# A decoder layer in split fp32: the high halves of 16 up-projection chunks come by a casting DMA of GpSimd's

## The chip, the cores and the metric

One core of a Trainium2 chip runs one launch of the kernel; the other cores are idle. The metric is the device time of one execution in microseconds (us), and for the kernel before it is the median of 2 runs. Profiles are of one execution each. Engines are named PE (TensorE, matmuls), ACT (ScalarE), DVE (VectorE), POOL (GpSimd) and SP (SyncE, which here only issues DMAs). PEld is TensorE's loading of its stationary operand.

## The reference, cut to what matters

One layer of a hybrid decoder over 256 tokens of width 1024, float32 in and out: a mixer of two branches (a chunkwise matrix memory and block attention), a layer norm, a gated feed-forward block, and a second layer norm. The change touches the feed-forward block:

```python
def conv_gated_mlp(x, w_up, conv_ffn, w_down):
    u = causal_dwconv(jnp.einsum("bsd,df->bsf", x, w_up), conv_ffn)
    g, up = jnp.split(u, 2, axis=-1)
    return jnp.einsum("bsf,fd->bsd", jax.nn.silu(g) * up, w_down)

# reference(), for its one layer
x = layer_norm(ALPHA * x + mix, ln1_g[l], ln1_b[l])
ffn = conv_gated_mlp(x, w_up[l], conv_ffn[l], w_down[l])
x = layer_norm(ALPHA * x + ffn, ln2_g[l], ln2_b[l])
```

`w_up` is 1024 x 5632 (gate and value, 2816 columns each), `w_down` 2816 x 1024, and the convolution is causal with three taps per channel.

## The kernel before, in words

**Split operands.** Matmuls run on float32r operands, a rounded form of float32. To keep float32 accuracy, each operand is cut in two: a high half, the value cast to float32r, and a low half, the value minus its high half. One product is three matmuls (`mm3`, L126: high x high L129, and the two mixed products L130 and L131). `split_into` (L91) makes the halves: ACT casts the high half (L93), DVE subtracts to get the low half (L94).

**Chunks.** All weights come from HBM as one stream of chunks of 128 partitions x 2048 float32 (1 MiB, 8 KB for each partition), in the order of `chunk_order` (L45). An "up" chunk holds 128 gate columns and 128 value columns of `w_up`; there are 22, up 0 to up 21. A "dn" chunk holds 256 rows of `w_down`; there are 11. From up 4 on they go in rounds: dn 0, up 4, up 5, dn 1, up 6, up 7, and so on to dn 7, up 18, up 19, and then up 20, up 21, dn 8, dn 9, dn 10. The first matmuls of dn d take the hidden chunks of up 2d and 2d + 1.

**Buffers.** `load` (L84) issues one chunk's DMA on SP's queue into a `raw` tile; there are three raw tiles, three `wh` tiles (high halves) and three `wl` tiles (low halves). `split_parts` (L100) takes a raw tile and a pair of `wh` and `wl`, cuts the 2048 columns into pieces (two of 1024 for most chunks), and returns one closure for each piece that calls `split_into`. A tile's next user waits until the last reader of the previous one is done: for `wh` and `wl` that is the matmuls of the chunk three before.

**The main loop** (in `run`) takes one chunk s per step. It emits the elementwise work of the step before and the split of chunk s + 2, then the load of chunk s + 5, then the matmuls of chunk s:

```python
self.elem_work(s, [] if late else self.split_parts(s + 2))
self.load(s + 5)
...
getattr(self, "step_" + kind)(s, i)
```

The order on each engine is the order of emission; every engine runs its own list and waits on semaphores. In a step after an up chunk the elementwise list is `[conv, None, None, gate]`, and the two pieces of the split take the places of the two `None`. `conv` is two ACT scalings (L1045) out of PSUM and four DVE multiply-adds (L1049). `gate` is a Silu on ACT (L1056), a product on DVE (L1057), and the split of the hidden chunk into `hh` (ACT) and `hl` (DVE). In a step after a dn chunk there is only the split.

**GpSimd** has few instructions here: two DMAs for the rows of the second layer norm (`load_ln_rows`, L843, emitted in the gate of up 5) and a power with one column in each layer norm (L949).

Of the kernel before, what the change touches and what calls it, by code (L numbers as in the profile page):

```python
# [10 lines left out]
F32 = mybir.dt.float32  # L11
F32R = mybir.dt.float32r
# [6 lines left out]
P = 128  # L19
# [13 lines left out]
WCOLS = KT * 264 + 64  # L33
# [27 lines left out]
def shift(kind, i):  # L61

    if kind in ("vm", "vb", "o"):
        return 48
    if kind in ("wa", "wb"):
        return 56
    if kind == "dn":

        return 40
    return 0 if kind == "wo" else 16  # L70


class Kernel:
# [10 lines left out]
    def load(self, s):  # L84
# [3 lines left out]
        self.nc.sync.dma_start(t, self.wst[s])  # L88
        self.raw[s] = t

    def split_into(self, wh, wl, raw):  # L91

        self.nc.scalar.copy(wh, raw)  # L93
        self.nc.vector.tensor_sub(wl, raw, wh.bitcast(F32))  # L94
# [5 lines left out]
    def split_parts(self, s):  # L100
        if s >= len(self.order) or s in self.w:
            return []
        raw = self.raw.pop(s)
        if s in self.extra:
            wh, wl = self.extra.pop(s)
            a = 8
        else:
            wh = self.stream.tile([P, WCOLS], F32R, tag="wh", name=f"wh{s}", bufs=3)
            wl = self.stream.tile([P, WCOLS], F32R, tag="wl", name=f"wl{s}", bufs=3)
            a = shift(*self.order[s])  # L110

        e, z, n, _ = odd(*self.order[s])
        wh, wl = (t[:, a - e:a + 2048 + z] for t in (wh, wl))
        edges = sorted({0, 256 if e else 0, 1024, 2048 - n, 2048})
        cuts = [(*(t[:, self.col(s, b):self.col(s, b) + d - b] for t in (wh, wl)), raw[:, b:d])
                for b, d in zip(edges, edges[1:])]
        self.w[s] = (wh, wl)
        return [lambda c=c: self.split_into(*c) for c in cuts]

    def col(self, s, c):  # L120
# [1027 lines left out]
def odd(kind, i):  # L1148

    if kind == "kb":  # L1150
        return 0, 8, 128, False
    if kind == "ga" and i < NG - 1:
        return 0, 8, 128, True
    if (kind, i) == ("up", 2):
        return 0, 8, 256, True
    if (kind, i) in (("vb", 3), ("up", 0), ("up", 1)):
        return 8, 0, 0, False
    return 0, 0, 0, False
# [78 lines left out]
```

## Time and profile before

| | |
|---|---|
| median of 2 runs | 486.95 us (486.84 to 487.06) |
| span of the profiled execution, first to last instruction | 484.5 us |
| granted TensorE clock, mean | 0.995 |
| busy: PE, PEld, DVE, ACT, POOL | 475.0, 459.4, 370.8, 288.1, 27.4 us |
| DMA moved | 94.29 MB, 195 GB/s over the span |

The profiled execution has a span only; its own time with what lies around the span isn't listed apart, and the median of the runs is 2.45 us above the span. A row of groups reads: line, engine, operation, output <- inputs, shapes, count | busy us, mean ns of one | idle time of the engine before them and what ended it. A row of the timeline gives start, length (us), engine, line, operation and count, and in brackets how long the engine stood idle before it and what released it. A row of DMA issues ends with the median us from issue to landing.

### The profile page before, as it was taken

How to read it: one execution, taken by the hardware profiler on the slowest of the kernel's cores; microseconds unless marked ns; L12 is line 12 of the kernel's file. 1: busy time of each engine (PE TensorE's matmuls, PEld its weight loads, DVE VectorE, ACT ScalarE, POOL GpSimd, SP SyncE). 2: the span in 40 equal slices, each digit the busy share in tenths (PEclk: the TensorE clock that was granted, in tenths of full speed). 3: DMA queues.
4: the chain of work that ended last, by engine and by line, in shares of the span. 5: the costliest groups of instructions: out<-in, count | busy, mean ns of one | idle time of the engine just before them, and what ended most of it. 6: DMA issues, size and time to landing. Idle time of an engine off the chain costs nothing.

```text
span 484.5 us, 9423 instructions
## 1 busy us (share of the span) xinstructions
PE 475.0 (98%) x3832; PEld 459.4 (95%) x3832; DVE 370.8 (77%) x681; ACT 288.1 (59%) x499; POOL 27.4 (6%) x43
## 2 busy tenths in 40 slices
PE   8999999999999999999999999999999999999993
PEld 6999999999999999999999999999999999999983
DVE  4877986897689668985677798878668666866877
ACT  5578876686667666866654623766456545654530
POOL 0501011001100110002000001000000000000000
PEclk9999999999999999999999999999999999999998
DMA  7986676375536562653954581827464545465202
GB/s 219 315 295 178 219 264 202 114 268 191 212 116 244 193 211 93 239 203 112 379 206 173 180 342 45 305 87 261 175 224 170 215 175 197 172 220 192 88 1 88
DMA packets 20918, 94.29 MB, mean 195 GB/s; under 512 B 4837, under 2 KB 7793, under 8 KB 11017
## 3 DMA queue, kind: packets, MB, share of 16 engines
q1 hardware_dynamic: 16714, 87.61, 50.9%
q0 software_dynamic: 4160, 6.07, 4.1%
q8 instruction: 30, 0.49, 0.4%
q14 instruction: 14, 0.11, 0.1%
HBM read 92.58 MB, written 2.64 MB: 197 GB/s over the span
## 4 chain that ended last, share of the span: by engine, by line
PE 97%; DMA 1%; DVE 1%; SPq 0%; issue 0%; ACT 0%; DVEq 0%
PE ps_up L131 8%; PE ps_up L129 8%; PE ps_up L130 8%; PE ffn L131 4%; PE ffn L130 4%; PE ffn L129 4%; PE ps_qm L129 2%; PE ps_vb L130 2%; PE ps_vb L131 2%; PE ps_vb L129 2%; PE ps_wb L131 2%; PE ps_ga L130 2%; PE mix L131 2%; PE ps_ga L131 2%; PE ps_kb L131 2%; PE ps_wa L131 2%
## 5 line engine op out<-in xcount | busy, mean ns | idle before, releaser
L94 DVE TENSOR_TENSOR wl<-raw,wh 128x1024 fp32r<-128x1024 f32 (+4 forms) x163 | 181.3, 1154 | 27.6 <-ACT wh L93 27.0
L93 ACT CAST wh<-raw 128x1024 fp32r<-128x1024 f32 (+4 forms) x163 | 153.1, 993 | 7.8 <-DMA raw<-in_wst_dram 4.6
L129 PE MATMUL ps_up<-x1h,wh 128*128 128x256 f32 x320 | 88.5, 277 | 0.0
L131 PE MATMUL ps_up<-x1h,wl 128*128 128x256 f32 x320 | 88.5, 277 | 0.0
L130 PE MATMUL ps_up<-x1l,wh 128*128 128x256 f32 x320 | 88.4, 276 | 0.0
L129 PEld LDWEIGHTS ps_up<-x1h,wh 128*128 128x128 f32 x320 | 60.2, 188 | 0.3
L130 PEld LDWEIGHTS ps_up<-x1l,wh 128*128 128x128 f32 x320 | 60.1, 188 | 0.4
L131 PEld LDWEIGHTS ps_up<-x1h,wl 128*128 128x128 f32 x320 | 60.1, 188 | 0.0
L1049 DVE SCALAR_TENSOR_TENSOR cu<-ps_up,vec,cu 128x255 f32<-128x255 f32 (+1 forms) x80 | 33.1, 476 | 23.5 <-ACT cu L1045 23.5
L131 PE MATMUL ffn<-wh,hl 128*128 128x512 f32 (+1 forms) x94 | 35.5, 378 | 0.0
L130 PE MATMUL ffn<-wl,hh 128*128 128x512 f32 (+1 forms) x94 | 35.5, 377 | 0.0
L129 PE MATMUL ffn<-wh,hh 128*128 128x512 f32 (+1 forms) x94 | 35.3, 375 | 0.0
L93 ACT CAST hh<-cu 128x256 fp32r<-128x256 f32 x22 | 8.9, 407 | 43.0 <-DVE cu L1057 43.0
L1045 ACT ACTIVATE cu<-ps_up,vec 128x256 f32<-128x256 f32 x40 | 16.7, 469 | 26.1 <-PE ps_up L131 26.1
L131 PEld LDWEIGHTS ffn<-wh,hl 128*128 128x128 f32 x94 | 17.7, 188 | 3.2
L130 PEld LDWEIGHTS ffn<-wl,hh 128*128 128x128 f32 x94 | 17.7, 188 | 3.1
L129 PEld LDWEIGHTS ffn<-wh,hh 128*128 128x128 f32 x94 | 17.7, 188 | 3.0
L129 PE MATMUL ps_qm<-xth,wh 128*128 128x256 f32 x64 | 18.1, 282 | 0.0
L129 PE MATMUL ps_ga<-xth,wh 128*128 128x256 f32 x64 | 18.0, 281 | 0.0
L129 PE MATMUL mix<-wh,mgh 128*128 128x256 f32 x64 | 17.8, 279 | 0.0
L129 PE MATMUL ps_vb<-wh,xth 128*128 128x256 f32 x64 | 17.8, 279 | 0.0
L130 PE MATMUL ps_vb<-wl,xth 128*128 128x256 f32 x64 | 17.8, 278 | 0.0
(319 smaller groups left out, 1437.8 us busy)
## 6 DMA issues: line engine op xcount, KB each, us to landing
raw<-in_wst_dram SPq DMA_DIRECT2D x77, 1024.0 KB, 4.8
raw<-in_wst_dram SPq DMA_DIRECT2D x8, 256.0 KB, 4.6
lnrow<-in_rows_dram POOLq DMA_DIRECT2D x4, 512.0 KB, 7.1
band<-table POOLq DMA_DIRECT2D x4, 384.0 KB, 12.7
xraw<-in_xt_dram SPq DMA_DIRECT2D x8, 128.0 KB, 4.2
toe<-band POOLq DMA_DIRECT2D x4, 256.0 KB, 3.7
xtok<-in_x_dram POOLq DMA_DIRECT2D x1, 1024.0 KB, 8.0
sgb<-in_wst_dram SPq DMA_DIRECT2D x4, 128.0 KB, 4.4
```

What stands on the lines that cost most here:

```text
L93: self.nc.scalar.copy(wh, raw)
L94: self.nc.vector.tensor_sub(wl, raw, wh.bitcast(F32))
L129: mm(ps, ah if first is None else first, bh, start=start, stop=False)
L130: mm(ps, ah, bl, start=False, stop=False)
L131: mm(ps, al, bh, start=False, stop=stop)
L1045: act.activation(cu[:, j, :], ps[:, j, :], AF.Copy, scale=tap(2, j))
L1049: v.scalar_tensor_tensor(cu[:, j, o:], ps[:, j, :S - o], tap(t, j), cu[:, j, o:], op0=ALU.mult, op1=ALU.add)
```

## The change

For the up chunks 6 to 21 (`by_cast`), ACT no longer casts the high half. `split_parts` takes the chunk's `wh` and `wl` tiles itself, and issues on POOL's queue a DMA from the chunk in HBM (`self.wst[s]`) straight into the 2048 columns of `wh`. The source is float32 and the destination float32r, so the transfer casts. The chunk is still loaded into its raw tile by SP as well, and each of the two closures is only the DVE subtraction, raw minus high half. The tiles go through `self.extra`, which holds pairs made ahead; the columns used (from 16 on) are those that `shift` gives for up chunks. The other chunks are as they were.

```diff
+    def by_cast(self, s):
+        kind, i = self.order[s]
+        return kind == "up" and i >= 6
+
...
         raw = self.raw.pop(s)
+        if self.by_cast(s):
+            wh = self.stream.tile([P, WCOLS], F32R, tag="wh", name=f"wh{s}", bufs=3)
+            wl = self.stream.tile([P, WCOLS], F32R, tag="wl", name=f"wl{s}", bufs=3)
+            self.nc.gpsimd.dma_start(wh[:, 16:2064], self.wst[s])
+            self.extra[s] = wh, wl
         if s in self.extra:
             wh, wl = self.extra.pop(s)
-            a = 8
+            a = 16 if self.by_cast(s) else 8
...
         self.w[s] = (wh, wl)
+        if self.by_cast(s):
+            return [lambda c=c: self.nc.vector.tensor_sub(c[1], c[2], c[0].bitcast(F32)) for c in cuts]
         return [lambda c=c: self.split_into(*c) for c in cuts]
```

## The prediction

> **What bounds the kernel now.** I read the page from the top: the busy shares, then the chain that ended last, then the stage that the change touches, by groups, by windows and by the timeline.
>
> ```profile
> span 484.5 us, 9423 instructions
> PE 475.0 (98%) x3832; PEld 459.4 (95%) x3832; DVE 370.8 (77%) x681; ACT 288.1 (59%) x499; POOL 27.4 (6%) x43
> ...
> PE 97%; DMA 1%; DVE 1%; SPq 0%; issue 0%; ACT 0%; DVEq 0%
> ```
>
> TensorE's matmuls fill 475.0 of 484.5 us, and 97% of the chain runs on TensorE. ACT, from which work is taken, is busy 59% and holds nothing of the chain. The next views are the chain in order of time (start, length, what) and stretches of one round (length, busy time of each engine with its instructions, granted clock, DMA share, GB/s).
>
> ```profile
> 367.70 0.23 PE ffn L129
> ...
> 384.08 0.23 PE ffn L129
> ...
> 433.22 0.23 PE ffn L129
> ...
> 460.48 0.23 PE ffn L129
> ```
>
> ```profile
> 346.10:362.48 16.38, 16.38 (x122) 15.39 (x122) 11.73 (x18) 8.69 (x15) 0.00 (x0) 1.00 0.54 193
> 362.48:378.86 16.38, 16.38 (x122) 15.39 (x122) 11.72 (x18) 8.68 (x15) 0.00 (x0) 1.00 0.54 194
> 378.86:395.24 16.38, 16.38 (x122) 15.39 (x122) 11.72 (x18) 8.69 (x15) 0.00 (x0) 1.00 0.55 195
> ```
>
> The down chunks start every 16.38 us (367.70, 384.08): one round is a down chunk and two up chunks, 5.46 us each. In a round TensorE is busy 16.38 of 16.38 us at clock 1.00, so in this stage no wait is left to remove. ACT is free for half of it, VectorE for 4.7 us, and the DMA engines are used to 0.55. A change here can gain next to nothing; the question is whether it makes a new wait.
>
> **The change, part by part.** What goes are two ACT casts per up chunk, for 16 chunks:
>
> ```profile
> L94 DVE TENSOR_TENSOR wl<-raw,wh 128x1024 fp32r<-128x1024 f32 x56 | 65.9, 1220 | 4.7 <-ACT wh L93 4.7
> L93 ACT CAST wh<-raw 128x1024 fp32r<-128x1024 f32 x55 | 54.9, 1049 | 0.0
> ```
>
> 32 x 1.049 = 33.6 us of ACT, all beside matmuls: worth 0 on the path. The 32 subtractions of 1.22 us stay, now behind a transfer instead of ACT. What comes are 16 DMA issues on POOL's queue and 16 MiB of traffic. Next in POOL's order after them stands only this:
>
> ```profile
> 471.35 0.66 POOL L949 TENSOR_TENSOR rs<-rs,mhalf 128x1 f32<-128x1 f32 x1 [170.78 <-DVE rs L948]
> ```
>
> and the two loads of the second normalisation's rows, which now stand behind the casts of up 6 and 7 and wait for the end of up 5 (about 334.9). They land over 100 us ahead of their use at 471. Cost 0.
>
> **The new wait.** The buffer of a high half has three copies, so the transfer for a chunk may start when TensorE has finished the chunk three before it. Up 12 as the example: up 10 ends at 367.70 + 2 x 5.46 = 378.62, and up 12 starts at 384.08 + 5.46 = 389.54. That leaves 10.92 us. VectorE's rows and ACT's in that stretch:
>
> ```profile
> 381.11 2.35 DVE L94 TENSOR_TENSOR wl<-raw,wh 128x1024 fp32r<-128x1024 f32 x2
> 383.38 0.42 DVE L1057 TENSOR_TENSOR cu<-cu 128x256 f32<-128x256 f32 x1
> 384.27 0.42 DVE L94 TENSOR_TENSOR hl<-cu,hh 128x256 fp32r<-128x256 f32 x1 [0.47 <-ACT hh L93]
> 385.01 1.65 DVE L1049 SCALAR_TENSOR_TENSOR cu<-ps_up,vec,cu 128x255 f32<-128x255 f32 x4 [0.31 <-ACT cu L1045]
> 386.57 2.35 DVE L94 TENSOR_TENSOR wl<-raw,wh 128x1024 fp32r<-128x1024 f32 x2
> ...
> 390.69 1.22 DVE L94 TENSOR_TENSOR wl<-raw,wh 128x1024 fp32r<-128x1024 f32 x1 [0.53 <-ACT wh L93]
> ```
>
> ```profile
> 378.67 0.84 ACT L1045 ACTIVATE cu<-ps_up,vec 128x256 f32<-128x256 f32 x2 [3.44 <-PE ps_up L131]
> ...
> 389.61 2.00 ACT L93 CAST wh<-raw 128x1024 fp32r<-128x1024 f32 x2
> ```
>
> Today up 12's subtractions run from 381.11 to 383.46, six us early. No row shows a casting transfer, so I bound it by the nearest: a plain MiB issued by SP, a plain MiB issued by GpSimd, and GpSimd's longest row load.
>
> ```profile
> raw<-in_wst_dram SPq DMA_DIRECT2D x77, 1024.0 KB, 4.8
> ...
> xtok<-in_x_dram POOLq DMA_DIRECT2D x1, 1024.0 KB, 8.0
> ```
>
> ```profile
> DMA to landing us min/median/max: 4.8/7.1/11.5
> ```
>
> Landing after issue: 4.8 us at best, 8.0 for the same size from GpSimd with two row loads and a raw chunk beside it, 11.5 for the slowest row load (the last fence is the row loads' own view). I take 6, between the first two, as only one other transfer is usually beside it. With 0.3 us (my estimate) for POOL to notice the end of up 10, it lands at 384.9, the subtractions end at 387.3, and TensorE wants the first at 389.5. The limit is 10.92 - 0.3 - 1.22 - 0.1 = 9.3 us. Only the first subtraction counts: of the 48 matmuls of an up chunk the first 12 read the first half of the columns, so the second is wanted 12 x 5.46/48 = 1.4 us later. At 8.0 it is still hidden.
>
> Behind the waiting subtraction stand on VectorE the product (L1057), the low half of the hidden chunk (L94 hl) and the next convolution (L1049). On ACT the cast of hh waits for the product, and behind it stand the next L1045 and the casts of the following down chunk (today 389.61). All slip by the same 3 to 6 us. Hidden chunks are first used a round later; the down chunk's subtractions, today 390.69 to about 393, would end at 396 to 399 and are needed at 384.08 + 16.38 = 400.46. SP's raw loads wait for the subtractions, slip as much, and have a round before use. So in a steady round the cost is 0.
>
> **The traffic.** The DMA engines must carry 5 MiB in a round where they carry 3: 5.24 MB in 16.38 us, 320 GB/s in place of the 193 to 195 above. What they reach in full use (two stretches of 1 us), and what the two queues took in all (packets, MB, share of 16 engines):
>
> ```profile
> 370.00:371.00 1.00, 1.00 (x7) 0.81 (x6) 1.00 (x2) 0.79 (x2) 0.00 (x0) 1.00 1.02 434
> 386.00:387.00 1.00, 1.00 (x6) 0.84 (x5) 1.00 (x3) 1.00 (x2) 0.00 (x0) 1.00 1.04 442
> ```
>
> ```profile
> q1 hardware_dynamic: 16714, 87.61, 50.9%
> q0 software_dynamic: 4160, 6.07, 4.1%
> ```
>
> A raw MiB (1.049 MB) costs all 16 engines 1.049/0.438 = 2.4 us at the peak, or 0.55 x 16.38/3 = 3.0 us by the share of a round. By GpSimd's queue it costs 4.1% x 484.5 = 19.9 us for 6.07 MB, or 3.4 us, with much smaller packets than a row of 8 KB. A round then needs 3 x (2.4 to 3.0) + 2 x 3.4 = 14.0 to 15.8 us of 16.38: it fits, without much room. The tightest place is the end, where up 18 to 21 follow one another: four casts and four raw loads in 4 x 5.46 = 21.84 us. At 2.4 all over they need 19.2, with 3.4 for a cast 23.2 to 25.6, so 0 to 3.8 us late.
>
> **Sum:** 0 (ACT) + 0 (rounds) + 0 to 3.8 (end); I take 1.5, nearer to the peak rows, since a cast's rows of 8 KB are like raw's. On the profiled execution that is 484.5 + 1.5 = 486.0 us of span. The median of the runs, 486.95, lies 2.45 us above the span; with it 488.5.
>
> **Rivals.**
> *The casting transfer moves at half the rate* (the other side: slower). Nothing in the trace speaks for it but that it has no cast; q0's 3.4 us speaks against it for plain transfers. A cast would take 4.8 to 6.0 us of the engines: a round 3 x 2.4 + 2 x 4.8 = 16.8 up to 21.0, so 0.4 to 4.6 over, six times: 2 to 28 us. The end needs 28.8 to 36, 7 to 14 over. Together 9 to 42, middle 25: 512 us. It decides from the point where a cast costs (16.38 - 3 x 2.4)/2 = 4.6 us of the engines.
> The Trainium skill (DMA: Bandwidth & Descriptors, section Bandwidth, measured table for transfers issued from GpSimd) gives 6.15 us of DMA time for 1 MB. By it a round would take 3 x 2.4 + 2 x 6.15 = 19.5 us and the kernel about 518; that is an estimate from the page, inside this rival, and the trace's plain transfers (2.4 to 3.4) disagree with it.
>
> *The transfer has the full rate but lands late.* GpSimd issues slowly:
>
> ```profile
> 228.64 0.74 POOL L837 DMA_DIRECT2D xtok<-in_x_dram  x1 [8.70 <-PE pso L789]
> ```
>
> The issue is 0.74 us and the landing up to 11.5. Each round then lasts 0.3 + L + 1.22 + 0.1 + 5.46 = L + 7.1 us, and past L = 9.3 every us costs one in each of about seven rounds: at 11.5, 7 x 2.2 = 15, so 490 to 504.
> The Trainium skill (SBUF — State Buffer, Who interferes with whom) says that a two-input VectorE instruction contends with a GpSimd instruction that reads SBUF, and that only transfers issued by GpSimd can be held up so. The subtractions are such instructions; two of them ahead of an issue (2.35 us) would bring a landing of 6 to 8.4, under 9.3, and one of 8.0 to 10.4, 1.1 over it: 7 x 1.1 = 8 us, 495 by this estimate. No row here shows it.
>
> *Faster:* TensorE has no gap in this stage, so this needs matmuls that run quicker without ACT's reads; no row suggests it.
>
> *It doesn't do what it says:* the transfer copies without rounding, so the low halves become zeros. The same instructions run: the forecast's time.
>
> **How the numbers follow.** Forecast, hidden or nearly (486.5 to 492): 0.58. Late landing (490 to 504): 0.12. Half rate (496 to 529): 0.22. Still slower (rows broken into short packets, a third of the rate or less, above 529): 0.06. Faster: 0.02. The predicted time is the likeliest case's, 488.5. The range starts at 486.3; upwards it takes in the late landing and half of the half rate, to 512, which leaves out about 0.19. Two per cent, about what a measurement of this kernel can tell from no change, is 9.7 us, so slower starts at 496.7: nearly all of the half rate (0.21), half of the late landing (0.06) and the rest (0.06) are slower, 0.33. Faster by that much is 0.01, and 0.66 is left for the same.
>
> **What would show it.** ACT's L93 wh group 32 instructions shorter, about 33 us less busy; 16 POOL issues with a landing of 5 to 8 us; VectorE's L94 waiting for a DMA instead of ACT; rounds still 16.38 us; the DMA share near 0.9 and 320 GB/s. I am wrong if casts land after more than 9.3 us, if the share stands at 1.0 with less than 320 GB/s, or if TensorE's matmuls of an up chunk wait for L94. A growth from round to round means traffic; the same amount in each round means landing.

## The result, and the profile after

The changed kernel takes 492.87 us (median of 2 runs, 492.82 to 492.92) where the kernel before took 486.95: ratio 1.0129, 95% interval [1.0113, 1.0146], 5.9 us slower. The profiled execution's span is 491.1 us, 6.6 longer. The page after (in the new file `mm3` is L140 to L142, `split_into` L97 and L98, the cast's issue L111, the lone subtraction L128):

```profile
span 491.1 us, 9436 instructions
PE 477.3 (97%) x3832; PEld 459.9 (94%) x3832; DVE 370.7 (75%) x681; ACT 258.8 (53%) x467; POOL 36.2 (7%) x59
...
PE 91%; DVE 3%; DMA 3%; issue 2%; ACT 1%; SPq 0%; DVEq 0%; ACTq 0%
```

ACT has lost 32 instructions and 29 us, POOL has 16 more. TensorE's share of the chain is down from 97% to 91%, and VectorE, the DMAs and "issue" (time in which an engine waits for nothing that the profile shows) have grown. The rounds first (columns as in the prediction: length, PE, PEld, DVE, ACT, POOL busy with counts, clock, DMA share, GB/s):

```profile
346.10:362.48 16.38, 16.38 (x122) 15.39 (x122) 10.69 (x17) 3.17 (x9) 1.06 (x2) 1.00 0.84 311
362.48:378.86 16.38, 16.38 (x122) 15.39 (x122) 11.82 (x18) 5.00 (x11) 1.06 (x2) 1.00 0.84 322
378.86:395.24 16.38, 16.38 (x122) 15.39 (x122) 11.73 (x18) 5.02 (x11) 1.06 (x2) 1.00 0.87 321
427.80:449.60 21.80, 21.80 (x170) 20.81 (x169) 13.62 (x22) 6.17 (x13) 2.12 (x4) 1.00 0.96 357
```

The rounds are still 16.38 us with TensorE full, at 311 to 322 GB/s and a DMA share of 0.84 to 0.87. Even in the 21.8 us in which the casts of up 18 to 21 and four raw loads are issued (the last row), at 0.96 and 357 GB/s, TensorE has no gap. All that it waits for in the down projection stands in three rows of the waits (total us, times, longest) and comes after 463:

```profile
PE ffn L141 <- DVE wl L98: 2.8, 2, 1.4
PE ffn L140 <- ACT wh L97: 1.6, 2, 0.8
...
PE ffn L140 <- ACT hh L97: 0.5, 1, 0.5
```

These are 4.9 us, and none of it is a wait for a cast: these are the high and low halves of down chunks 9 and 10, which ACT casts as before, and the last hidden chunk. The chain in order of time (start, length) shows where their lateness comes from:

```profile
444.43 8.09 DMA wh<-in_wst_dram
452.52 1.55 issue
...
455.22 1.22 DVE wl L128
456.43 0.35 DVE cu L1068
```

The cast of up 21, issued at 444.43, holds VectorE until 454.07. From there on VectorE works on to the last hidden chunk, with no pause but 0.3 to 0.5 us at a time for ACT's results, and TensorE follows. VectorE's end of the stage, before (L94, and the first row of the layer norm, L941) and after:

```profile
446.62 2.35 DVE L94 TENSOR_TENSOR wl<-raw,wh 128x1024 fp32r<-128x1024 f32 x2
...
463.03 2.35 DVE L94 TENSOR_TENSOR wl<-raw,wh 128x1024 fp32r<-128x1024 f32 x2
...
466.19 0.42 DVE L94 TENSOR_TENSOR hl<-cu,hh 128x256 fp32r<-128x256 f32 x1 [0.47 <-ACT hh L93]
468.04 0.69 DVE L941 SCALAR_TENSOR_TENSOR r<-x,ffn 128x512 f32<-128x512 f32 x1 [1.43 <-PE ffn L131]
```

```profile
436.76 2.36 DVE L128 TENSOR_TENSOR wl<-raw,wh 128x1024 fp32r<-128x1024 f32 x2 [3.15 <-issue]
...
448.59 2.36 DVE L128 TENSOR_TENSOR wl<-raw,wh 128x1024 fp32r<-128x1024 f32 x2 [2.77 <-DMA wh<-in_wst_dram]
...
454.07 2.36 DVE L128 TENSOR_TENSOR wl<-raw,wh 128x1024 fp32r<-128x1024 f32 x2 [1.55 <-issue]
...
459.55 2.35 DVE L98 TENSOR_TENSOR wl<-raw,wh 128x1024 fp32r<-128x1024 f32 x2
...
465.02 2.35 DVE L98 TENSOR_TENSOR wl<-raw,wh 128x1024 fp32r<-128x1024 f32 x2
...
473.65 0.43 DVE L98 TENSOR_TENSOR hl<-cu,hh 128x256 fp32r<-128x256 f32 x1 [0.47 <-ACT hh L97]
474.68 0.69 DVE L952 SCALAR_TENSOR_TENSOR r<-x,ffn 128x512 f32<-128x512 f32 x1 [0.59 <-PE ffn L142]
```

The subtractions of up 21 start at 454.07 in place of 446.62, 7.45 us late, and the last hidden chunk's low half is exactly as late (473.65 for 466.19). In between VectorE repeats a cycle of 5.47 us per chunk (459.55, 465.02), and TensorE takes 5.46 for one: VectorE makes up nothing. TensorE reads the last hidden chunk first at this matmul of the kernel before, and ACT had finished its high half one us earlier:

```profile
467.16 0.39 PE L129 MATMUL ffn<-wh,hh 128*128 128x512 f32 x1
```

```profile
465.75 0.41 ACT L93 CAST hh<-cu 128x256 fp32r<-128x256 f32 x1 [2.12 <-DVE cu L1057]
```

467.16 - 466.16 = 1.0 us was to spare, so 7.45 us of lag give some 6.5 of loss. The same matmul of the changed kernel:

```profile
473.68 0.50 PE L140 MATMUL ffn<-wh,hh 128*128 128x512 f32 x1 [0.49 <-ACT hh L97]
```

It starts 6.52 us later, and the span grew by 6.6. (The view counts 4.9 us of this as waits. By the starts of the matmuls, the sweep up to this one took 12.98 us in place of 6.84, and it began 0.38 us later.)

**Theory A (the end):** waiting for casts puts VectorE 4 to 9 us behind; in the rounds a chunk has reserve enough, but down chunks 8, 9 and 10 and the last hidden chunks are all wanted in one sweep over the first 128 tokens, and there the lag comes out. **Theory B (traffic):** 16 MiB more cost something each. Each timed run below has the kernel before beside it on the same chip, where it took 486.42 us (the first four runs) or 486.26 (the last four). Against these the changed kernel's 492.87 is some 6.5 us more, as the spans say; the 5.9 is against the two runs at 486.95.

### The profile page after: what moved, and what is told of

Same layout as the page of the kernel before. It is cut to its first block, busy times and chain, and to the rows that moved or that the text cites. A ratio compares the mean times of both kernels' runs of the same rounds, so it can differ in the third digit from the quotient of the medians.

```text
span 491.1 us, 9436 instructions
## 1 busy us (share of the span) xinstructions
PE 477.3 (97%) x3832; PEld 459.9 (94%) x3832; DVE 370.7 (75%) x681; ACT 258.8 (53%) x467; POOL 36.2 (7%) x59
## 3 DMA queue, kind: packets, MB, share of 16 engines
q1 hardware_dynamic: 16714, 87.61, 49.7%
q0 software_dynamic: 6464, 22.84, 13.1%
## 4 chain that ended last, share of the span: by engine, by line
PE 91%; DVE 3%; DMA 3%; issue 2%; ACT 1%; SPq 0%; DVEq 0%; ACTq 0%
PE ps_up L142 7%; PE ps_up L140 7%; PE ps_up L141 7%; PE ffn L140 4%; PE ffn L142 4%; PE ffn L141 4%; DMA wh<-in_wst_dram 2%; PE ps_qm L140 2%; PE ps_vb L142 1%; PE ps_vb L140 1%; PE mix L140 1%; PE ps_vb L141 1%; PE ps_ga L140 1%; PE ps_ga L141 1%; PE ps_wa L140 1%
## 5 line engine op out<-in xcount | busy, mean ns | idle before, releaser
L98 DVE TENSOR_TENSOR wl<-raw,wh 128x1024 fp32r<-128x1024 f32 (+4 forms) x131 | 143.5, 1137 | 27.7 <-ACT wh L97 27.1
L97 ACT CAST wh<-raw 128x1024 fp32r<-128x1024 f32 (+4 forms) x131 | 121.3, 979 | 8.9 <-DMA raw<-in_wst_dram 6.2
L142 PE MATMUL ps_up<-x1h,wl 128*128 128x256 f32 x320 | 88.7, 277 | 0.0
L140 PE MATMUL ps_up<-x1h,wh 128*128 128x256 f32 x320 | 88.5, 277 | 0.0
L140 PEld LDWEIGHTS ps_up<-x1h,wh 128*128 128x128 f32 x320 | 60.2, 188 | 0.3
L142 PEld LDWEIGHTS ps_up<-x1h,wl 128*128 128x128 f32 x320 | 60.1, 188 | 0.2 <-DVE wl L128 0.2
L128 DVE TENSOR_TENSOR wl<-raw,wh 128x1024 fp32r<-128x1024 f32 x32 | 37.7, 1220 | 27.7 <-issue 21.2
L97 ACT CAST hh<-cu 128x256 fp32r<-128x256 f32 x22 | 8.9, 406 | 74.4 <-DVE cu L1068 74.4
L140 PE MATMUL ffn<-wh,hh 128*128 128x512 f32 (+1 forms) x94 | 35.6, 379 | 2.1 <-ACT wh L97 1.6
L142 PE MATMUL ffn<-wh,hl 128*128 128x512 f32 (+1 forms) x94 | 35.6, 378 | 0.0
L1067 ACT ACTIVATE cu<-cu 128x256 f32<-128x256 f32 x22 | 9.2, 419 | 29.2 <-DVE cu L1060 29.2
L140 PEld LDWEIGHTS ffn<-wh,hh 128*128 128x128 f32 x94 | 17.7, 188 | 6.2 <-ACT wh L97 2.4
L142 PEld LDWEIGHTS ffn<-wh,hl 128*128 128x128 f32 x94 | 17.7, 188 | 3.2 <-DVE hl L98 0.2
L111 POOL DMA_DIRECT2D wh<-in_wst_dram x16 | 8.5, 533 | 138.2 <-PE ps_up L142 112.3
L140 PE MATMUL ps_qm<-xth,wh 128*128 128x256 f32 x64 | 18.1, 282 | 0.0
L140 PE MATMUL ps_ga<-xth,wh 128*128 128x256 f32 x64 | 18.0, 281 | 0.0
L140 PE MATMUL mix<-wh,mgh 128*128 128x256 f32 x64 | 17.8, 279 | 0.0
```

Source lines behind the costliest of these rows:

```text
L111: self.nc.gpsimd.dma_start(wh[:, 16:2064], self.wst[s])
L128: return [lambda c=c: self.nc.vector.tensor_sub(c[1], c[2], c[0].bitcast(F32)) for c in cuts]
L140: mm(ps, ah if first is None else first, bh, start=start, stop=False)
L142: mm(ps, al, bh, start=False, stop=stop)
L1067: act.activation(cu[:, 0, :], cu[:, 0, :], AF.Silu)
```

## The experiments

**Which casts cost: the first 12, the last 4, or 14 of 16.** Three versions of one line:

```diff
-        return kind == "up" and i >= 6
+        return kind == "up" and 6 <= i < 18      # first 12
+        return kind == "up" and i >= 18          # last 4
+        return kind == "up" and 6 <= i < 20      # 6 to 19
```

> Theory A (the end): VectorE falls behind the chunks by 4 to 9 us while it waits for casts; in the rounds that is covered, and only the last three down chunks, all wanted within one sweep with some 0.7 us to spare, make it visible. Without casts for up 18 to 21 VectorE should be back to about 1.0 us late at up 21, so 0.3 us of loss: 487.0 to 487.6. Theory B (traffic or casts cost something each, 5.9 us over 16): 12 casts leave 4.4 us, 491.4.

Measured: 486.36 us, ratio 1.0009 [0.9996, 1.0022]. Twelve casts cost nothing that can be measured. Up 21's subtractions, 7.45 us late in the changed kernel, are 0.5 late in this one:

```profile
447.15 2.35 DVE L98 TENSOR_TENSOR wl<-raw,wh 128x1024 fp32r<-128x1024 f32 x2
```

> Theory A: the last four casts alone, less crowded before them, make up 21's subtractions about 6 to 7.5 us late, less 0.7: 5.2 to 6.7 us of loss, 491.5 to 493.5. Theory B (5.9 us spread over 16 casts): 1.5 us, 488.4.

Measured: 490.55 us, ratio 1.0075 [1.0055, 1.0095], 3.7 us by the ratio (2.7 to 4.6). Four casts cost more than the 1.5 that B says, and less than the 5.2 to 6.7 that I expected of A: the place is A's, the size was missed. Up 21's subtractions were less late than expected:

```profile
453.03 2.36 DVE L128 TENSOR_TENSOR wl<-raw,wh 128x1024 fp32r<-128x1024 f32 x2 [4.16 <-issue]
```

That is 6.4 us after 446.62, but this trace ran 0.8 us late from before the first down chunk on, so the lag is 5.6; less the 1.0 to spare it gives 4.6.

> Up 20 and 21 are cast by ACT again. Theory A: followed along the rows, VectorE's subtractions of up 21 start 3.9 us later than in the kernel before (450.5 for 446.6), less 0.7 to spare: 3.2 us of loss, 489.7 to 490.6. Theory B: 14 of 16 casts, 5.2 us, 492.1.

Measured: 489.12 us, ratio 1.0055 [1.0040, 1.0070], 2.7 us: A's side, a little under its 3.2. Its profile also has one cast that came late in a round. Up 8's landed after 10.4 us, past the 9.3 that the prediction worked out, and TensorE did wait for its subtraction (the first row is this run's):

```profile
PE ps_up L142 <- DVE wl L128: 0.8, 1, 0.8
```

```profile
PEld ps_up L142 <- DVE wl L128: 0.2, 1, 0.2
```

The two up chunks of that round took 12.0 us of TensorE in place of 10.9: the 1.1 us by which the cast passed 9.3. In the changed kernel the casts of the rounds stayed below the limit (8.6 at most); only the last two, 9.4 and 9.6, passed it. The second row is from there, and TensorE's four up chunks at the end took 22.06 us in place of 21.77, 0.3 more. So the limit is where the working put it.

**The same traffic, issued early.** The high halves of the cast chunks go to four tiles that are free in this stage (`ahead`, used only by up 0 and 1), so a cast waits for the chunk four up chunks before it, not for the chunk three before it in the stream.

```diff
-            wh = self.stream.tile([P, WCOLS], F32R, tag="wh", name=f"wh{s}", bufs=3)
+            wh = self.ring[self.order[s][1] % 4]
...
+                self.ring = [t for j in range(2) for t in self.extra[first["up"] + j]]
```

> All 16 casts and all their traffic stay, but their high halves go into four tiles of their own (free in this stage), so a cast can be issued up to two rounds ahead instead of two chunks. Theory A: every cast has landed before VectorE comes to it, the lag at up 21 is 0, and the time is that of the kernel before within 0.5 us: 486.5 to 487.5. Theory B: the traffic is the same, so the loss stays, 492 to 493.

Measured: 490.40 us, ratio 1.0080 [1.0065, 1.0095]. By the time alone this is B's result, but the profile says that it is neither. No TensorE instruction of the stage waits for anything, and yet a round lasts 16.9 us:

```profile
L130 PE MATMUL ps_up<-x1l,wh 128*128 128x256 f32 x160 | 44.2, 276 | 0.0
```

```profile
L141 PE MATMUL ps_up<-x1l,aheadl 128*128 128x256 f32 x80 | 22.7, 283 | 0.0
```

The first row is the kernel before, the second this one (the same product, x1's low half with the high half of the weights, which lies in the tile named `aheadl` here), both over the stretch 340 to 420: the up matmuls themselves are slower. ACT's first reads show an up chunk of 5.72 us in place of 5.46, and 16 x 0.26 = 4.2 us is the loss (3.9 by the ratio). The traffic is not what slows them, since the last up chunk still takes 5.72 us when nothing is transferred (DMA share 0.00):

```profile
458.78:464.50 5.72, 5.72 (x51) 5.72 (x49) 4.68 (x8) 3.44 (x7) 0.00 (x0) 1.00 0.00 0
```

What else had changed is where the tiles lie: in the compiled program the high halves began 32 bytes past a multiple of 256, in the ordinary tiles 128 past one. So the same again, 24 columns (96 bytes) further:

```diff
-            wh = self.ring[self.order[s][1] % 4]
+            wh = self.ring[self.order[s][1] % 4][:, 24:2112]
```

> The same as the run with four own tiles, but the high halves start at column 40 of those tiles, where their address stands to x1h's as in the ordinary tiles (there the up chunks took 5.72 us of matmuls in place of 5.46, with no wait before any). Theory A (VectorE's lag at the end is all of the loss, and the slower matmuls of the run before came from the address): rounds of 16.38 us again, no lag, 0 to 0.4 us of loss, 486.2 to 486.9 against a kernel before of 486.4. Theory B (traffic slows the matmuls themselves): rounds stay at 16.9 us, 490.4.

Measured: 486.15 us, ratio 0.9997 [0.9988, 1.0006]. All 16 casts, all their traffic, and no loss:

```profile
362.48:378.86 16.38, 16.38 (x122) 15.39 (x121) 11.72 (x18) 5.13 (x10) 1.05 (x2) 1.00 0.85 321
```

```profile
447.05 2.35 DVE L128 TENSOR_TENSOR wl<-raw,aheadl 128x1024 fp32r<-128x1024 f32 x2
```

The same 321 GB/s as in the changed kernel's rounds, 16.38 us, and up 21's subtractions start without a wait. That rules out B, and since nothing else differs, the slow matmuls of the run before come from where the high halves begin. Why a place is slow stays open. Casts issued early undo the whole loss, and the kernel is level with the one before; since TensorE is full, nothing is won beyond that.

**The same waits without the traffic.** The raw loads of the cast chunks are left out (their low halves are then x1 minus the high half, so the kernel no longer computes the layer).

```diff
     def load(self, s):
+        if self.by_cast(s):
+            self.raw[s] = self.x1.rearrange("p t d -> p (t d)")
+            return
```

> The raw loads of the 16 cast chunks are left out (the subtraction reads x1 in their place), so the DMA engines carry 3 MiB a round again, and the wait for the cast stays. Theory A: casts land 5.1 to 5.5 us after issue in place of 7.9 (9.6 for the last), up 21's subtractions start 3 us late in place of 7.5, less 0.7 to spare: 2.0 to 2.7 us of loss, 488.4 to 489.1. Theory B (the traffic alone): no loss. If the cast itself is what is slow: landing still near 8 and 4 us or more of loss.

Measured: 488.25 us, ratio 1.0039 [1.0024, 1.0054], 1.9 us. The casts of this run, and those of the changed kernel (the view of the tile wh):

```profile
DMA to landing us min/median/max: 5.0/5.2/7.8
```

```profile
DMA to landing us min/median/max: 5.3/7.9/9.6
```

With 3 MiB in a round, as before the change, a cast lands after 5.2 us, where a raw MiB from SP took 4.8: the cast itself is not slow. Up 21's subtractions start 2.7 us later than in the kernel before (446.62), and less the 1.0 to spare that is 1.7 of the 1.9:

```profile
449.35 2.36 DVE L131 TENSOR_TENSOR wl<-x,wh 128x1024 fp32r<-128x1024 f32 x2 [1.36 <-DMA wh<-in_wst_dram]
```

So about a third of the loss is the wait for any transfer at all, and the other two thirds go with the raw loads, beside which a cast takes 8 to 10 us.

**VectorE late, with no transfer.** The kernel before; VectorE repeats one subtraction of a chunk six times.

```diff
+        if self.order[s] == ("up", 21):          # or 13
+            ...
+                for _ in range(6):
+                    self.nc.vector.tensor_sub(l, r, h.bitcast(F32))
```

> The kernel before with no casting transfer, and VectorE repeats the first subtraction of up 21 six times: 6 x 1.13 = 6.8 us late there. Theory A: a delay of VectorE alone gives the loss, 6.8 less 0.7 = 6.1 us, 492.0 to 493.0 against 486.4. Theory B (needs the transfers): no loss or 1 us.

Measured: 493.74 us, ratio 1.0155 [1.0137, 1.0172], 7.5 us. The repeats took more than I had reckoned:

```profile
448.65 7.53 DVE L124 TENSOR_TENSOR wl<-raw,wh 128x1024 fp32r<-128x1024 f32 x6
```

7.53 less 1.0 is 6.5; the interval, 6.7 to 8.4 us, begins just above it. A delay of VectorE alone, with no casting transfer, gives the whole loss and somewhat more. Where the rest comes from isn't shown; in the profiled execution TensorE was 0.8 us late before the first down chunk already, and its clock fell to 0.50 between 469 and 471.

> The same six repeats at up 13. Theory A: in a round VectorE has 4.7 us to spare and TensorE's next chunks are ready, so the lag is gone two rounds on: 0 loss, within 0.4 us of the kernel before. If any delay of VectorE counted, 6 us.

Measured: 486.83 us, ratio 1.0012 [1.0002, 1.0021], 0.6 us (0.1 to 1.0), just past the 0.4 expected. In the profile up 13's own matmuls wait 0.4 us for their second piece, which stood behind the repeats. Of VectorE's lag behind TensorE's chunks 4.2 us are left at up 14, 1.2 at up 16, and none at up 18. The same repeats cost 7.5 us at the end and next to nothing in the rounds.

## Why the prediction was right and where it was off

The size was 5.9 us where 1.5 was forecast, inside the range and inside 2%, but just above the likeliest case's own stretch (to 492). The range reached higher for the sake of rivals that did not come true, so that it held is in part luck. Step by step:

- **ACT's 33.6 us are worth 0:** right. 29 us of ACT went, and with the casts issued early the time is level with the kernel before (ratio 0.9997).
- **The new wait is hidden in the rounds:** right, with the limit of 9.3 us where it was put. Its 0.3 for POOL to notice fits: an issue came at 384.35, and TensorE began the chunk after the one waited for at 384.01. The landing was mis-sized: 6 was taken, 7.9 was measured, because the prediction reckoned one other transfer beside a cast and the rounds, at 0.84 of the DMA engines, have more (without the raw loads of the cast chunks it was 5.2).
- **The traffic fits:** right. GpSimd's queue went from 4.1% of 484.5 us to 13.1% of 491.1: 44.5 us for 16 casts, 2.8 us of all engines each, where 2.4 to 3.4 was the bound. A raw MiB took 49.7% of 491.1 over 83.6 MiB, 2.9 us. That ends the rival of half rate. The 6.15 us that the Trainium skill (DMA: Bandwidth & Descriptors, Bandwidth) gives for 1 MB does not hold here as a cost to the DMA engines; the measured 2.8 decides.
- **"0 to 3.8 (end)":** this is the step that failed. It found the right place and weighed the wrong thing there. It counted engine time of the DMA for four casts and four raw loads; that was all but covered, and TensorE lost 0.3 us up to 460. What counted was VectorE's lag, 7.45 us at up 21, which the prediction had worked out itself ("all slip by the same 3 to 6 us") and let go because in a round everything has a chunk or more of reserve. It never asked what has a reserve when the rounds end: in the sweep over three down chunks it was 1.0 us, and the other 6.5 were lost.
- **Late landing** as a rival had the mechanism of a late transfer, and its price was right: what a cast landed past 9.3 was lost (1.1 us at up 8 in the run of 14 casts). But in the changed kernel no cast of the rounds was that late, so they lost nothing.
- **The rule on VectorE and GpSimd** (the Trainium skill, SBUF — State Buffer, Who interferes with whom): the 16 issues took 0.53 us each, shorter than the 0.74 of the plain load of x, of the same size, before; no issue was seen to be held up. The same section of the Trainium skill adds, which the prediction left out, that `tensor_tensor`, the operation of these subtractions, did not stall a DMA when it was probed; these issues agree with that.

That the growth of the landing (7.3 us at up 10 to 9.6 at up 21) comes from the raw loads drifting into the casts is argued, not tested by itself.

## What to carry to other kernels

An engine that runs behind costs nothing while each consumer has reserve, and its lag is paid in full where the stream ends: work out the reserve of the last chunks by themselves before you call a wait hidden. Where an engine's cycle is as long as the bound engine's (5.47 against 5.46 us here), it cannot make up what it has lost. A transfer that replaces an instruction needs a buffer that is free one transfer earlier; with four tiles for the casts alone, the same casts cost nothing.

## What the runs showed of the hardware

- **The pace of matmuls changed with where the stationary tile begins:** the up chunk took 5.72 us with the high halves 32 bytes past a multiple of 256, and 5.46 us with them 128 past, with x1h and x1l 64 past. Only these two places were tried, and the reason isn't known.
- **A casting transfer runs at the plain rate:** float32 to float32r cost 2.8 us of the 16 engines per MiB, where a raw MiB cost 2.9, and landed after 5.2 us in rounds of 3 MiB in all.
- **TensorE's granted clock fell to 0.50 among the gaps at the end** in two profiles, of the last four casts (between 471 and 473) and of VectorE's repeats at up 21 (between 469 and 471). In the changed kernel's profile, with gaps as long, it stayed at 1.00, so the gaps alone don't decide it. The first two rows are the last four casts, the third the changed kernel:

```profile
469.00:471.00 2.00, 0.62 (x2) 0.30 (x3) 2.00 (x4) 1.03 (x2) 0.00 (x0) 0.91 0.00 0
471.00:473.00 2.00, 2.00 (x5) 1.49 (x5) 1.53 (x3) 0.41 (x1) 0.00 (x0) 0.50 0.00 0
```

```profile
471.00:473.00 2.00, 1.23 (x5) 0.86 (x5) 2.00 (x3) 0.09 (x1) 0.00 (x0) 1.00 0.00 0
```
